# A batched matrix product: output stores joined two by two, on the semaphores of the first loads

## Chip, core and metric

The kernel runs on one core of one Trainium2 chip. The metric is the device time of one execution in microseconds, as a median of several. Profiles are of one execution each; the profile's span is some 1.7 us shorter than the time of the same execution (before: 121.65 us of 123.40 us). Kernels are compared only within the same rounds. PE is TensorE, DVE VectorE, ACT ScalarE, POOL GpSimd, and SP the sync engine, which issues all DMAs.

## The reference

```python
def setup_inputs():
    batch, m, k, n = 16, 512, 512, 512
    return {"a": np.random.randn(batch, k, m).astype(np.float32),
            "b": np.random.randn(batch, k, n).astype(np.float32)}

def reference(a, b):
    return np.matmul(a.transpose(0, 2, 1), b).astype(np.float32)
```

Two inputs of 16.8 MB each come in and one output of 16.8 MB goes out, 50.33 MB in all.

## The kernel before

Batches are handled in eight pairs. A pair's a and b are loaded in fp32 (2 MB each, four buffers), cast to bf16 by DVE, multiplied by PE into PSUM, and copied by ACT into one of seven output buffers (such a copy is called an eviction). The eighth pair reuses the first output buffer, so ACT waits there for the first store. SP issues every load, then every store, on one queue.

```python
out_v = out.rearrange("(pair g) (c t) n -> pair c g t n", g=G, t=T)   # G = 2, T = 4
NO = pairs - 1                                                        # 7 output buffers
o_ts = [pool.tile([P, G, T, N], f32, name=f"o{j}") for j in range(NO)]
# ... loads; the last one is issued in two halves, the first of them on s_h
nc.sync.wait_ge(s_h, 16)
for i in range(pairs - 1):
    nc.sync.wait_ge(s_out, i + 1)              # ACT has finished pair i
    nc.sync.dma_start(out_v[i], o_ts[i % NO][:]).then_inc(s_o if i else s_o0, 16)
# ... casts on DVE, matmuls on PE
for i in range(pairs):                         # ACT
    if i == NO:
        nc.scalar.wait_ge(s_o0, 16)            # first store landed: buffer 0 is free
    # ... four copies PSUM -> o_ts[i % NO], then s_out += 1
with tc.tile_critical(sync_engine=mybir.EngineType.Pool, no_gpsimd_drain=True):
    nc.gpsimd.wait_ge(s_o0, 16)
    nc.gpsimd.wait_ge(s_o, 16 * (pairs - 2))
tc.no_sync_barrier()
nc.sync.dma_start(out_v[pairs - 1], o_ts[(pairs - 1) % NO][:])        # final store
```

## Time and profile before

| what | value |
|---|---|
| time, median of 3 runs | 123.24 us (123.08 to 123.38) |
| span of the profiled execution | 121.65 us |
| busy share: PE, DVE, ACT | 53%, 31%, 26% |
| share of the 16 DMA engines' span filled with packets | 97.8% |
| DMAs: loads, stores | 19, 8 |
| data packets: 16 KB (loads), 8 KB (part of the loads, all stores) | 1664, 2816 |

What matters in the table is not how busy a compute engine is, but that the DMA engines have no idle time to give back. Every DMA also writes one small semaphore packet on each of the 16 engines; 27 DMAs make the 432 small packets of the page. Below, a boundary is the place on one engine where one DMA's semaphore packet ends it and the next DMA's data begin, and the receipt is the time from the last of these packets to the complete semaphore.

### The profile page before, as it was taken

Reading aid. Unit: us, or ns where it says so; the run is one execution under the profiler, and the core shown is the slowest. Engines: PE = TensorE matmul, PEld = TensorE weight load, DVE = VectorE, ACT = ScalarE, POOL = GpSimd, SP = SyncE. Lnnn points to the kernel's source line nnn. Section 1 sums busy time; section 2 is a strip of 40 time slices with the busy share of each in tenths; the row PEclk is TensorE's granted clock in tenths of the full one; section 3 lists DMA queues with packets and bytes.
Section 4 is the critical chain, followed back from the end, with each engine's and each line's share of the span. In section 5 each row is a group of like instructions: output and inputs, shape, how many; then the busy total and the mean of one; then the engine's idle time right before and its main releaser. Section 6 shows DMA issues by size and latency. Waiting matters only on the chain. (4 is left out here: it accounts for less than half of the span.)

```text
span 121.7 us, 1207 instructions
## 1 busy us (share of the span) xinstructions
PE 65.0 (53%) x480; PEld 35.6 (29%) x480; DVE 38.0 (31%) x48; ACT 32.2 (26%) x41; POOL 0.2 (0%) x4
## 2 busy tenths in 40 slices
PE   0007937919989759739969919999930000000000
PEld 0002302306646336414536605556610000000000
DVE  0051061095684094082464446266000000000000
ACT  4000330330390840840191480065190000000000
POOL 0000000000000000000000000000000000000000
PEclk9999996799999999976999996899999555555555
DMA  3999999999999999999999999999999999999993
GB/s 59 428 428 426 463 431 431 431 431 436 431 431 431 431 431 431 431 431 431 431 431 431 431 431 399 431 420 423 426 428 423 428 431 431 431 431 428 431 428 162
DMA packets 4912, 50.33 MB, mean 414 GB/s; under 512 B 432, under 2 KB 432, under 8 KB 432
## 3 DMA queue, kind: packets, MB, share of 16 engines
q1 hardware_dynamic: 4912, 50.33, 97.8%
HBM read 33.55 MB, written 16.78 MB: 414 GB/s over the span
## 5 line engine op out<-in xcount | busy, mean ns | idle before, releaser
L151 PE MATMUL ps<-bbf,abf 64*128 64x512 bf16 x448 | 53.1, 394 | 11.9 <-PEq L146 11.9
L151 PEld LDWEIGHTS ps<-bbf,abf 64*128 64x128 bf16 x448 | 31.4, 113 | 33.7 <-issue 19.2
L176 ACT COPY o<-ps 128x1024 f32<-128x1024 f32 x28 | 26.3, 1026 | 39.3 <-PE ps L151 39.3
L113 DVE CAST abf<-x 128x2048 bf16<-128x2048 f32 x14 | 17.2, 1225 | 20.6 <-PE ps L151 14.9
L113 DVE CAST bbf<-x 128x2048 bf16<-128x2048 f32 x14 | 17.1, 1224 | 11.8 <-DMA x<-in_b_dram 11.8
L131 PE MATMUL ps<-bbf,abf 128*128 128x512 bf16 x32 | 11.9, 554 | 12.5 <-PEq L129 12.5
L131 PEld LDWEIGHTS ps<-bbf,abf 128*128 128x128 bf16 x32 | 4.3, 138 | 19.6 <-issue 19.1
L170 ACT COPY o<-ps 128x1024 f32<-128x1024 f32 x4 | 4.1, 1014 | 19.2 <-PE ps L131 19.2
L94 DVE CAST abf<-x 128x2048 bf16<-128x2048 f32 x2 | 2.5, 1228 | 12.7 <-PE ps L131 6.9
L94 DVE CAST bbf<-x 128x2048 bf16<-128x2048 f32 x2 | 2.5, 1226 | 1.2 <-DMA x<-in_b_dram 1.2
L181 ACT ACTIVATE done<-done 1x1 uint32<-1x1 uint32 x8 | 1.6, 197 | 0.0
L170 ACT ACT_TABLE_LOAD x1 | 1.3, 1283 | 0.9 <-SPq L69 0.9
L119 DVE MEMSET done<- 1x1 f32 x14 | 0.8, 59 | 0.0
L98 DVE MEMSET done<- 1x1 f32 x2 | 0.1, 59 | 0.0
L203 POOL MEMSET const-uint8-127<- 128x1 uint8 x1 | 0.1, 103 | 0.0
L203 POOL MEMSET const-bfloat16-1.0<- 128x1 bf16 x1 | 0.1, 102 | 0.0
L203 POOL MEMSET const-float32-0.0<- 128x1 f32 x1 | 0.1, 99 | 0.2 <-issue 0.2
L203 POOL MEMSET const-float32-1.0<- 128x1 f32 x1 | 0.1, 99 | 0.0
## 6 DMA issues: line engine op xcount, KB each, us to landing
out_dram<-o SPq DMA_DIRECT2D x8, 2048.0 KB, 22.2
x<-in_a_dram SPq DMA_DIRECT2D x7, 2048.0 KB, 12.1
x<-in_b_dram SPq DMA_DIRECT2D x6, 2048.0 KB, 15.6
x<-in_b_dram SPq DMA_DIRECT2D x4, 1024.0 KB, 12.1
x<-in_a_dram SPq DMA_DIRECT2D x2, 1024.0 KB, 6.8
```

The costliest lines, as they stand in the source:

```text
L94: nc.vector.tensor_copy(out=bf_ts[0][:], in_=x_ts[j][:, u * RV:(u + 1) * RV, :]).then_inc(s_cast, 1)
L98: nc.vector.memset(dve_done[:, j:j + 1], 0.0).then_inc(s_in, 1)
L113: nc.vector.tensor_copy(out=(bbf_ts if n % 2 else abf_ts)[v][:], in_=x_ts[n % NX][:, v * RV:(v + 1) * RV, :],).then_inc(s_cast, 1)
L119: nc.vector.memset(dve_done[:, n:n + 1], 0.0).then_inc(s_in, 1)
L131: mm = nc.tensor.matmul(ps_ts[0][h][:, t % 2, :], a_m[:, r, t], bbf_ts[0][:, r, :], start=(r == 0), stop=(r == RV - 1),)
L151: mm = nc.tensor.matmul(ps_ts[g][h][:, t % 2, :], a_m[:, t], bbf_ts[v][rows, r, :], start=(v == 0 and r == 0), stop=(v == V - 1 and r == R ...
L170: nc.scalar.copy(out=o_ts[0][:, g, 2 * h:2 * h + 2, :], in_=ps_ts[0][h][:]).then_inc(s_ev[h], 1)
L176: ev = nc.scalar.copy(out=o_ts[i % NO][:, g, 2 * h:2 * h + 2, :], in_=ps_ts[g][h][:])
L181: nc.scalar.memzero(act_done[:, i:i + 1]).then_inc(s_out, 1)
L203: nc = _bacc.Bacc("TRN2", target_bir_lowering=False, num_devices=1)
```

## The change

Its intent is fewer and larger DMAs (two pairs, 4 MB, per store) and two semaphores fewer: the stores count on the semaphores on which the first two loads landed. The output buffers become slices of one tile, so that two neighbours are contiguous in a partition.

```diff
-    out_v = out.rearrange("(pair g) (c t) n -> pair c g t n", g=G, t=T)
+    out_v = out.rearrange("batch (c t) n -> c batch t n", t=T)
...
-    o_ts = [pool.tile([P, G, T, N], f32, name=f"o{j}") for j in range(NO)]
+    o_t = pool.tile([P, NO, G, T, N], f32, name="o")
+    o_ts = [o_t[:, j] for j in range(NO)]
...
     s_f = [tc.alloc_semaphore(f"s_f{j}") for j in range(2)]
+    s_o0, s_o = s_f
-    s_o0 = tc.alloc_semaphore("s_o0")
-    s_o = tc.alloc_semaphore("s_o")
...
-        for i in range(pairs - 1):
-            nc.sync.wait_ge(s_out, i + 1)
-            nc.sync.dma_start(out_v[i], o_ts[i % NO][:]).then_inc(s_o if i else s_o0, 16)
+        for i in range(0, NO, 2):
+            n = min(2, NO - i)
+            nc.sync.wait_ge(s_out, i + n)
+            nc.sync.dma_start(
+                out_v[:, G * i:G * (i + n)],
+                o_t[:, i:i + n].rearrange("p i g t n -> p (i g) t n"),
+            ).then_inc(s_o if i else s_o0, 16)
...
-                nc.scalar.wait_ge(s_o0, 16)
+                nc.scalar.wait_ge(s_o0, 32)
...
-        nc.gpsimd.wait_ge(s_o0, 16)
-        nc.gpsimd.wait_ge(s_o, 16 * (pairs - 2))
+        nc.gpsimd.wait_ge(s_o0, 32)
+        nc.gpsimd.wait_ge(s_o, 16 * ((NO + 1) // 2))
...
-    nc.sync.dma_start(out_v[pairs - 1], o_ts[(pairs - 1) % NO][:])
+    nc.sync.dma_start(out_v[:, batch - G:batch], o_ts[(pairs - 1) % NO])
```

## The prediction

> **What bounds the kernel now.** I began with the page's slices. The rows below are TensorE, ScalarE, the mean busy share of the 16 DMA engines in tenths, and what they moved. The reader is to see that the compute engines are idle for the last quarter, and that the DMA row has no hole between its first and last slice.
>
> ```profile
> PE   0007937919989759739969919999930000000000
> ACT  4000330330390840840191480065190000000000
> DMA  3999999999999999999999999999999999999993
> GB/s 59 428 428 426 463 431 431 431 431 436 431 431 431 431 431 431 431 431 431 431 431 431 431 431 399 431 420 423 426 428 423 428 431 431 431 431 428 431 428 162
> ...
> q1 hardware_dynamic: 4912, 50.33, 97.8%
> ```
>
> The queue line puts one number on it: packets occupy 97.8% of the span, on one queue, for 50.33 MB. What the change can win is therefore not in PE, DVE or ACT, but in (a) the two ends of the span and (b) whatever the queue loses between one DMA and the next. The second view was the time line of the issuing engine (SP), together with the waits of that engine. Columns of the time line: start, duration, line, operation.
>
> ```profile
> 65.72 0.43 SPq L82 DMA_DIRECT2D x<-in_b_dram  x1
> 78.82 10.87 SPq L87 DMA_DIRECT2D out_dram<-o  x7
> 91.68 2.63 SPq L188 DMA_DIRECT2D out_dram<-o  x1
> ...
> SPq L214 <- DMA out_dram<-o: 26.3, 1, 26.3
> SPq L87 <- DMA x<-in_b_dram: 12.6, 1, 12.6
> SPq L87 <- ACT done L181: 0.5, 1, 0.5
> ```
>
> The loads are all issued by 66.2 us. SP then waits 12.6 us for the first half of the last load, issues seven stores back to back from 78.82 us, and the eighth at 91.68 us. After that, SP sits 26.3 us waiting for that eighth store to land: in the last quarter the kernel only drains a queue that was filled long before. The view of the output tensor gives issue times (least, median, greatest, in ns):
>
> ```profile
> L87 SPq DMA_DIRECT2D out_dram<-o x7: 403/1262/4927, 78.8 to 84.8; - x7
> L188 SPq DMA_DIRECT2D out_dram<-o x1: 2628/2628/2628, 91.7 to 91.7; - x1
> DMA to landing us min/median/max: 7.5/22.2/31.1
> ```
>
> An issue costs 0.40 us when the queue has room, and up to 4.93 us when it must wait for room. 4.93 us is one store's own transfer time: the sequencer is held up by a full queue, the queue is not held up by the sequencer. The third view was a table of stretches; the last two columns are DMA share and rate.
>
> ```profile
> 3.00:78.00 75.00, 53.98 (x384) 29.02 (x386) 33.25 (x42) 23.24 (x30) 0.00 (x0) 0.93 1.01 430
> 81.00:86.00 5.00, 4.65 (x44) 2.68 (x42) 2.37 (x4) 2.92 (x5) 0.00 (x0) 1.00 0.99 419
> 86.00:91.00 5.00, 3.38 (x32) 1.97 (x28) 0.00 (x0) 3.28 (x4) 0.00 (x0) 1.00 1.03 434
> 101.00:106.00 5.00, 0.00 (x0) 0.00 (x0) 0.00 (x0) 0.00 (x0) 0.00 (x0) 0.50 1.02 433
> 106.00:111.00 5.00, 0.00 (x0) 0.00 (x0) 0.00 (x0) 0.00 (x0) 0.00 (x0) 0.50 1.02 431
> ```
>
> The load phase runs at 430 GB/s and five-microsecond stretches of the store phase at 419 to 434 (stretches this short scatter with the packets that happen to cross their edges). So loads of 2 MB and stores of 2 MB both keep the engines full, with a DMA boundary every 4.9 us.
>
> Finally I read the trace's packet records themselves. One DMA engine starts an 8192 B data packet every 306 ns. At the end of each store it writes one 4 B semaphore packet, and the next data packet starts **6 ns** after that one (80.541 us, then 80.547 us on the engine that ends its loads first). Boundaries on one engine are 4.900 us apart, again and again (85.441, 90.341, 95.241 us): 16 packets at 305.9 ns, 4.894 us, and 6 ns. That is the whole visible cost of a DMA boundary.
>
> **What the Trainium skill says.** "DMA: Bandwidth & Descriptors", section "Anatomy of one DMA", gives a fixed cost of about 2 us per DMA (fitted on the GpSimd path), mostly the receipt of the last write, and says that the semaphore write itself is a bubble of about one cycle. The trace agrees on the second point (6 ns). The receipt is there too, but short and hidden: the last semaphore packet starts at 120.333 us and the semaphore is complete at 120.708 us, 0.375 us, and between stores it runs beside the next store's data. "SBUF — State Buffer", section "The DMA setup-cost knee", advises coalescing into the largest transfer; its formula for 2 MB would give 2 + 4.81 = 6.8 us, but here stores come 4.90 us apart, because the DMAs are queued. That rule is the change's intent and does not apply here. "DMA: Bandwidth & Descriptors", section "Where 436 GB/s comes from", has a ceiling of 435 GB/s; the trace's 431 GB/s is within 1% of it, so a larger DMA has next to no rate left to gain. The section on why a DMA increments its semaphore by 16 warns of two DMAs in flight on one semaphore. Here the first loads have long landed (5.8 and 8.2 us) before a store adds to the same semaphores (after 85 us), and every wait is for the full sum (32, or 64 for one load and three stores), so the reuse is safe and costs no time.
>
> **The change part by part.**
> Stores: in place of seven loop stores there are three of 4 MB and one of 2 MB; the final 2 MB store stays, so eight DMAs become five. On the DRAM side each partition still has runs of 4 x 512 floats, 8192 B, as in the trace's records of the stores; only four such runs instead of two belong to a partition. So I keep 2048 data packets of 8192 B and 128 per engine. Removed: 3 boundaries x 6 ns = **0.02 us** on every engine. Removed from SP: three issues of 0.4 to 1.3 us, off the path.
> Start of the stores: the first 4 MB store needs the output of pairs 0 and 1, ready long before. The wait for the first half of the last load still comes last and passes at 78.82 us. At the kernel's start the first data packet followed its issue by 1.02 us (0.942 to 1.961 us). A store issued at 78.82 us could thus move data from 79.84 us, and the first engine to finish its loads gets to it at 80.541 us: 0.7 us of slack. Issues of 128 packets took 0.33 to 0.44 us and of 256 packets 0.40 us, so I take 0.5 us, 0.8 at most, for 512, which fits in the slack. Cost 0.
> ScalarE: its last four evictions reuse the first output buffer and wait for the first store. That landed at 86.32 us, before the matmuls were ready at 87.67 us. After the change they wait for a store of 4 MB, which lands where the second store lands today, 91.42 us. The evictions move from 87.72 to about 91.5 us, take 3.76 us as today, and the final store is issued at about 95.5 us instead of 91.68. Its first data packet is due at about 115 us, when four loop stores (14 MB) have drained. Slack: some 18 us. Cost 0.
> Semaphores: two fewer. The one instruction that clears them all at the end takes 0.16 us; I count at most 0.01 us for two.
> End: the slowest engine's last packet, the receipt (0.375 us), and the closing barriers (0.94 us from 120.708 to the span's end) stay. Sum: -0.02 - 0.01 = **-0.03 us**, so 123.21, rounded to **123.2 us**.
>
> **The rivals.**
> First, *each DMA pays a fixed cost in the open*. If the 2 us of the skill were paid at every boundary, three fewer would give about 6 us, 117 us. Against it: next data 6 ns after the semaphore packet, on all engines. If only the 0.375 us receipt were paid, 1.1 us and 122.1 us; the same records speak against it.
> Second, *a new hole between loads and stores*. If descriptors of a 4 MB store take twice as long and start only when all are made, the slack of 0.7 us could be used up. At 1.3 us of issue (the worst of the stores that waited in part) it would be overrun by about 0.2 us: 123.4 us.
> Third, *the late eviction becomes the bound*. This needs 18 us of further delay; I see nothing that would make it. Were the store and eviction serialised at the end, the final 2 MB would stand alone: some 5 us, 128 us.
> Fourth, *one engine's luck*. From the last boundary of the loads, 80.900 us, eight stores of 4.900 us end at 120.100 us. Fifteen engines keep that schedule; one, which should have ended at 120.033, ends at 120.333 us, since its packets between 83 and 92 us took 315 to 352 ns instead of 309. That is 0.23 us on the end of the span, in the stretch in which SP issues into a full queue. With other issues this can vanish (123.0 us) or grow (123.4 us). It is larger than all that the change removes.
> Fifth, *other addresses of the writes*: a partition's four runs lie in four batches, 1 MB apart, instead of two. Two at the same distance run at full rate today; I give a slower write of some per cent a chance of one in fifty.
>
> **Range and chances.** The three runs of before lie within 0.3 us. The fourth rival gives 0.2 us either way, the second 0.2 upwards. The range is 122.95 to 123.5 us. A change of 2% would be 2.5 us, which only the first rival (down) or the third and fifth (up) could make: 0.01 and 0.02; same 0.97.
>
> **What would show it right or wrong.** Right: 2048 store packets still of 8192 B and 48 fewer small ones; DMA packets near 97.8% of the span and no dip between 80 and 82 us; the last evictions at about 91.5 us and the final issue at about 95.5 us with the end unmoved; landings of 4 MB stores some 9.8 us apart. Wrong: store packets of another size or longer than 309 ns throughout; a stretch with idle DMA engines near 81 us or 115 us; a final store that starts after the queue has run dry.

## The result

The kernel after took 123.19 us (median of 6 runs, 123.09 to 123.41), the kernel before, in the same rounds, 123.26 us (6 runs, 123.08 to 123.38). The ratio is 0.9998, with a 95% interval from 0.9985 to 1.0011: the same time. Ratios and intervals here are from the same rounds alone; they are not quite the ratios of the medians quoted.

The page of the kernel after has these rows: ACT, the DMA engines' busy share and rate by slice, and the queue's sum.

```profile
ACT  4000423302900920390560084190009200000000
...
DMA  2999999999999999999999999999999999999994
GB/s 57 424 432 429 467 432 432 432 432 432 432 432 432 432 432 427 432 432 416 432 427 427 432 432 402 432 427 427 429 429 432 429 429 432 421 424 429 429 424 208
...
q1 hardware_dynamic: 4864, 50.33, 97.7%
```

Still no hole in the DMA row between the ends. 48 packets fewer (4864 for 4912), which is the three removed DMAs times 16 engines, and the same bytes. In the ACT row the last evictions stand about a slice further right than before.

The time line of SP (start, duration, line, operation) and its waits:

```profile
65.65 0.43 SPq L83 DMA_DIRECT2D x<-in_b_dram  x1
78.75 8.98 SPq L89 DMA_DIRECT2D out_dram<-o  x4
95.04 0.37 SPq L193 DMA_DIRECT2D out_dram<-o  x1
```

```profile
SPq L219 <- DMA out_dram<-o: 24.9, 1, 24.9
...
SPq L89 <- DMA x<-in_b_dram: 12.6, 1, 12.6
```

The stores still go out when the first half of the last load has landed (78.75 us). Only the final store moved, from 91.68 to 95.04 us, and since the queue had room by then, it took 0.37 us to issue in place of 2.63. SP's wait for it is 24.9 us in place of 26.3, because it begins later and the span is 0.3 us shorter. The issue times of the stores (least, median, greatest, ns), and ACT's last copies on the time line (the bracket is the idle time before them and what ended it):

```profile
L89 SPq DMA_DIRECT2D out_dram<-o x4: 403/688/5502, 78.8 to 82.2; - x4
L193 SPq DMA_DIRECT2D out_dram<-o x1: 372/372/372, 95.0 to 95.0; - x1
...
DMA to landing us min/median/max: 12.3/25.4/33.3
```

```profile
91.09 3.76 ACT L181 COPY o<-ps 128x1024 f32<-128x1024 f32 x4 [8.88 <-DMA out_dram<-o]
94.71 0.20 ACT L186 ACTIVATE done<-done 1x1 uint32<-1x1 uint32 x1
```

The first 4 MB store takes 403 ns to issue, as the first 2 MB store did. ACT now waits 8.88 us for that store, and it costs nothing: the final store, which waits for ACT, is issued at 95.04 us and has to stand in the queue until 115 us in any case. A few stretches of the kernel after (us, then PE, PEld, DVE, ACT and POOL busy, granted clock, DMA share, GB/s):

```profile
3.00:78.00 75.00, 52.33 (x399) 29.54 (x401) 34.48 (x43) 23.24 (x30) 0.00 (x0) 0.95 1.01 431
...
81.00:86.00 5.00, 5.00 (x49) 3.09 (x47) 1.52 (x4) 1.21 (x3) 0.00 (x0) 1.00 1.02 433
86.00:91.00 5.00, 1.67 (x16) 0.83 (x12) 0.00 (x0) 0.00 (x0) 0.00 (x0) 1.00 1.00 424
```

Loads and stores run at the rates of before; the scatter of the store stretches is that of packets at their edges.

The packet records say it exactly. On one engine a 4 MB store takes 9.794 us from semaphore packet to semaphore packet, against 2 x 4.900 = 9.800 us for two 2 MB stores. The change removes 6 ns per removed boundary.

### The profile page after: what moved, and what is told of

Its sections match the earlier page's. It is cut to its first block, busy times and chain, and to the rows that moved or that the text cites. A ratio compares the mean times of both kernels' runs of the same rounds, so it can differ in the third digit from the quotient of the medians.

```text
span 121.4 us, 1204 instructions
## 1 busy us (share of the span) xinstructions
PE 61.7 (51%) x480; PEld 35.0 (29%) x480; DVE 38.1 (31%) x48; ACT 32.2 (27%) x41; POOL 0.2 (0%) x4
## 2 busy tenths in 40 slices
DMA packets 4864, 50.33 MB, mean 415 GB/s; under 512 B 384, under 2 KB 384, under 8 KB 384
## 3 DMA queue, kind: packets, MB, share of 16 engines
q1 hardware_dynamic: 4864, 50.33, 97.7%
## 4 chain that ended last, share of the span: by engine, by line
DMA 63%; DVE 6%; issue 3%; ACT 2%; SPq 2%; ACTq 1%
DMA x<-in_b_dram 53%; DMA out_dram<-o 10%; DVE bbf L118 3%; DVE abf L118 3%; ACT o L181 2%; SPq L74 1%; ACTq L70 1%; SPq L72 1%; SPq L80 0%; DVE done L124 0%; ACT done L186 0%; SPq L219 0%; SPq L70 0%
## 5 line engine op out<-in xcount | busy, mean ns | idle before, releaser
L181 ACT COPY o<-ps 128x1024 f32<-128x1024 f32 x28 | 26.3, 1026 | 45.9 <-PE ps L156 37.0
L136 PE MATMUL ps<-bbf,abf 128*128 128x512 bf16 x32 | 8.7, 433 | 12.4 <-PEq L134 12.4
L136 PEld LDWEIGHTS ps<-bbf,abf 128*128 128x128 bf16 x32 | 3.7, 121 | 16.9 <-issue 14.8
```

What stands on the lines that cost most here:

```text
L136: mm = nc.tensor.matmul(ps_ts[0][h][:, t % 2, :], a_m[:, r, t], bbf_ts[0][:, r, :], start=(r == 0), stop=(r == RV - 1),)
L181: ev = nc.scalar.copy(out=o_ts[i % NO][:, g, 2 * h:2 * h + 2, :], in_=ps_ts[g][h][:])
```

## Experiments

**Theory:** the kernel's time is the DMA queue's, a boundary between two queued DMAs costs 6 ns, and all other effects of the change have slack. **Rivals:** each DMA pays its completion in the open; the larger first store leaves a hole after the loads; the later eviction becomes the bound; single slow packets of one engine move the end, because SP issues into a full queue. Each kernel is the kernel before or after with the edit shown (the counts waited for on the store semaphores are adapted, which is not always shown); all gave correct results. The time after "beside" and the ratio refer to the kernel before in the same rounds.

### The semaphores alone (a_sem_only)

```diff
     s_f = [tc.alloc_semaphore(f"s_f{j}") for j in range(2)]
+    s_o0, s_o = s_f
-    s_o0 = ...; s_o = ...            # and the waits raised by 16 each
```

> The kernel before with the second part of the change alone: the store semaphores are those of the first loads, eight stores of 2 MB stay. Theory (the queue sets the time and no semaphore lies on its path): same, 123.2 us, within 0.1 us of before; the clearing instruction at the end at most 0.01 us shorter. Rival (a shared semaphore delays something, or fewer semaphores shorten the end): a difference above 0.2 us.

Measured: 123.39 us (5 runs) beside 123.36 us of before (9 runs), ratio 1.0001 (0.9988 to 1.0015). The clearing instruction took 161 ns in the kernel before and 158 ns in the kernel after. Within this interval the semaphores cost and win nothing.

### The 4 MB stores alone (b_4mb_only), and two repeats (after2, b2_4mb_only)

```diff
-    s_o0, s_o = s_f
+    s_o0 = tc.alloc_semaphore("s_o0")
+    s_o = tc.alloc_semaphore("s_o")   # and the waits lowered by 16 each
```

> The kernel after with its own store semaphores back: the 4 MB stores alone. Theory (a boundary between DMAs costs 6 ns of each engine): same, 123.2 us, with 27 DMAs less 3 and the slowest engine at its schedule of 9.794 us per 4 MB. Rival (each DMA's receipt is paid in the open, hidden in the change by a loss elsewhere that the semaphores cause): 1.1 us faster than before.

Measured: 123.18 us beside 123.36 us, ratio 0.9987 (0.9973 to 1.0001). The 1.1 us of the open receipt are excluded, but 0.13% is more than 0.02 us. So this kernel and the kernel after were run again, on one chip in the same rounds.

> The kernel after once more, with five rounds. The 4 MB stores alone came out 0.13% faster than before, with an interval that just holds 1. Theory (6 ns per boundary; the rest is which engine meets slow packets): within 0.1% of before, 123.2 us. Rival (4 MB stores are really some 0.2 us faster): 0.15% below before here and in the repeat of the 4 MB stores alone.

> The 4 MB stores with their own semaphores once more, on the same chip as the repeat of the kernel after. Theory: within 0.1% of before. Rival (a real gain of the 4 MB stores): again 0.13% or more below before.

Measured: the kernel after 123.25 us, ratio 0.9996 (0.9982 to 1.0010); the 4 MB stores with their own semaphores 123.19 us, ratio 0.9986 (0.9973 to 1.0000); before 123.33 us (9 runs). Neither text is met in full: the stores with their own semaphores were again 0.14% below before, outside the theory's 0.1%, while the kernel after, with the very same stores, was 0.04% below. Each interval alone just reaches 1, but both runs, on two chips, gave the same 0.13 to 0.14%, and all ten executions took 123.28 us or less. So a gain of some 0.15 us is more likely real than noise. The three boundaries give 0.02 us of it; the rest, and why the kernel after does not show it, stays unexplained. It is small beside the 2% (2.5 us) that would count.

### More DMAs instead of fewer (c_1mb)

```diff
-            nc.sync.dma_start(out_v[i], o_ts[i % NO][:]).then_inc(...)
+            for g in range(G):
+                nc.sync.dma_start(out_v[i][:, g], o_ts[i % NO][:, g]).then_inc(...)
```

> The kernel before with each loop store split by batch: fourteen stores of 1 MB and the final one of 2 MB, 15 stores in place of 8, packets still 8192 B. Theory of 6 ns per boundary: 7 x 6 ns = 0.04 us more, so 123.3 us, same. Rival of the open receipt (0.375 us per DMA): 2.6 us more, 125.8 us. Rival of 2 us per DMA: 14 us more.

Measured: 123.44 us beside 123.36 us, ratio 1.0013 (0.9999 to 1.0027). Seven more DMAs do not cost 2.6 us, let alone 14. On one engine the 1 MB stores are 2.453 us apart: eight packets at 305.9 ns and again 6 ns. The view of the output tensor shows what the sequencer does with it:

```profile
L88 SPq DMA_DIRECT2D out_dram<-o x14: 347/1218/1246, 78.8 to 93.2; - x14
L189 SPq DMA_DIRECT2D out_dram<-o x1: 831/831/831, 94.9 to 94.9; - x1
```

The typical issue takes 1.2 us, since the queue is full, and all the same the time is unchanged: SP has 2.45 us per store.

### More and smaller packets (h_4kb)

```diff
+            for h in range(H):
                 nc.sync.dma_start(
-                    out_v[:, G * i:G * (i + n)],
+                    out_v[:, G * i:G * (i + n), 2 * h:2 * h + 2],
-                    o_t[:, i:i + n].rearrange(...),
+                    o_t[:, i:i + n, :, 2 * h:2 * h + 2].rearrange(...),
                 ).then_inc(...)
```

> The kernel after with each loop store split by halves of a partition's rows: runs of 4096 B in place of 8192, so 1792 more data packets, 112 more on each engine, in eight loop DMAs and a final one. Theory (what costs is a packet, not a DMA): from 16 KB packets (607 ns apart, from 4.862 us per 2 MB load) against 8 KB packets (305.9 ns apart) one packet more costs about 4.8 ns, so 112 x 4.8 = 0.54 us more than after: 123.7 us. Rival (neither DMA count nor packet size matters at this rate): 123.2 us.

Measured: 123.73 us; the 4 MB stores of the same rounds took 123.18 us, so 0.55 us for 0.54 expected. Against before the ratio is 1.0029 (1.0016 to 1.0043). The page's packet and queue lines:

```profile
DMA packets 6721, 50.33 MB, mean 413 GB/s; under 512 B 449, under 2 KB 449, under 8 KB 4033
...
q1 hardware_dynamic: 6720, 50.33, 98.2%
```

The queue has 1856 packets more than in the kernel after: 1792 of data, and 64 semaphore packets of four more DMAs. 2 MB in 4 KB packets take 4.975 us on an engine (32 x 155.3 ns and 6 ns), in 8 KB packets 4.900 us: 4.7 ns for each packet more. The length of a contiguous run in the output is what cost time here, and the change leaves that at 8192 B.

### A first store of 8 MB (d_8mb) and of 12 MB (e_12mb)

```diff
-        for i in range(0, NO, 2):
-            n = min(2, NO - i)
+        for i, n in [(0, 4), (4, 3)]:        # d_8mb;  e_12mb: [(0, 6), (6, 1)]
```

> The kernel after with stores of four and three pairs (8 MB and 6 MB) and the final 2 MB. Theory (the wait of the last eviction for the first store has slack): the first store lands at about 100.9 us, the final store is issued at about 104.9 us and its data are due at 114.8 us, so no loss: 123.2 us. Rival (a late eviction costs time): a later end in proportion, some 10 us.

> The kernel after with one store of six pairs (12 MB), one of 2 MB and the final 2 MB. Theory: the first store lands at about 110.6 us, the final store is issued 3.98 us later as in the kernel after, at 114.6 us, and its first data come 1.02 us later, at 115.6 us; the engines run dry from 114.8 to 115.2 us, so a hole of some 0.5 to 0.9 us opens: 123.7 to 124.1 us. Rival (slack is larger, since data are handed on before the whole store has landed): 123.2 us.

Measured for 8 MB: 123.30 us beside 123.32 us, ratio 1.0000 (0.9985 to 1.0015). ACT's last copies and the final issue came another 10 us later than in the kernel after, at no cost:

```profile
101.16 3.76 ACT L180 COPY o<-ps 128x1024 f32<-128x1024 f32 x4 [18.83 <-DMA out_dram<-o]
...
105.12 0.37 SPq L192 DMA_DIRECT2D out_dram<-o  x1
```

Measured for 12 MB: 123.74 us, ratio 1.0037 (1.0021 to 1.0052). Now the slack is used up. The time line, then the stretches around 115 us:

```profile
110.80 3.76 ACT L180 COPY o<-ps 128x1024 f32<-128x1024 f32 x4 [26.91 <-DMA out_dram<-o]
...
114.75 0.37 SPq L192 DMA_DIRECT2D out_dram<-o  x1
```

```profile
113.00:115.00 2.00, 0.00 (x0) 0.00 (x0) 0.00 (x0) 1.61 (x3) 0.00 (x0) 0.50 0.93 393
115.00:115.60 0.60, 0.00 (x0) 0.00 (x0) 0.00 (x0) 0.00 (x0) 0.00 (x0) 0.50 0.04 14
115.60:118.00 2.40, 0.00 (x0) 0.00 (x0) 0.00 (x0) 0.00 (x0) 0.00 (x0) 0.50 1.03 437
```

The final store is issued at 114.75 us, as worked out beforehand; between 115.0 and 115.6 us the engines move next to nothing (DMA share 0.04), and the first packets of the final store start at 115.64 us. This is the third rival, real, but three times as far away as the change goes.

### The first store issued too late (f_late_first) and very early (i_early, j_one_early)

```diff
-        nc.sync.wait_ge(s_h, 16)
+        nc.sync.wait_ge(s_x[(2 * pairs - 1) % NX], 16 * (2 * pairs // NX))   # f_late_first
                                       # i_early: the line is taken away
+            if i: nc.sync.wait_ge(s_h, 16)                                   # j_one_early: in the loop
```

> The kernel after, in which the first store is issued only when the last load has landed in full (81.2 us) and not its first half (78.7 us). Theory (a store's data come 1.0 us after its issue, and only the early issue hides that): first data at about 82.2 us, loads drained at 80.5 to 80.9 us, so a hole of 1.4 to 1.7 us: 124.7 us. Rival (the engines work on at once, or the store phase is not what sets the end): 123.2 us.

Measured: 124.76 us beside 123.32 us, ratio 1.0122 (1.0107 to 1.0138). Stretches around the end of the loads, first of the kernel after, then of this one:

```profile
78.00:80.50 2.50, 2.15 (x22) 1.20 (x20) 1.57 (x2) 2.11 (x3) 0.00 (x0) 1.00 1.05 442
80.50:82.20 1.70, 1.70 (x16) 0.95 (x16) 1.70 (x3) 1.70 (x3) 0.00 (x0) 1.00 0.95 400
```

```profile
80.50:82.20 1.70, 1.70 (x16) 0.97 (x16) 1.70 (x3) 1.70 (x3) 0.00 (x0) 1.00 0.11 43
82.20:84.00 1.80, 1.80 (x18) 1.18 (x18) 0.33 (x2) 0.02 (x1) 0.00 (x0) 1.00 1.01 410
```

The 0.95 of the kernel after is no hole: the stretch before it has 1.05, the kernel before has 1.07 from 80.5 to 82.2 us, and in the packet records data follow each semaphore packet there within 6 ns. In this run the engines stand at 0.11 from 80.5 to 82.2 us, and each of them has a gap of 1.27 to 1.56 us, for 1.4 to 1.7 expected. The store was issued at 81.231 us and its first data packet started at 82.175 us, 0.94 us later. So the second rival's hole exists when the lead is missing; the change keeps the lead, and its 4 MB store is issued as fast as one of 2 MB.

> The kernel after without the issuing engine's wait for the first half of the last load before the first store, so that the first stores queue up right behind the loads. Theory (the lead of 2.4 us is already enough, the queue works in order): 123.2 us, no dip at 81 us and none before. Rival (a store's data delay the last loads or the queue's room is taken from them): later last loads and a longer time. If the lead were still too short, this would be faster.

Measured: 124.17 us beside 123.33 us, ratio 1.0071 (1.0057 to 1.0085). The theory's expectation failed here. The stretches:

```profile
78.00:80.50 2.50, 2.50 (x26) 1.70 (x24) 2.05 (x2) 0.36 (x1) 0.00 (x0) 1.00 1.02 334
80.50:82.20 1.70, 1.36 (x14) 0.61 (x10) 0.61 (x2) 1.70 (x3) 0.00 (x0) 1.00 0.98 400
```

Packets fill the engines (share 1.02), yet they move only 334 GB/s from 78 to 80.5 us: single 8 KB packets of the last half load took up to 872 ns for 309, and that load was complete at 82.20 us instead of 81.18. After that the stores ran on the usual schedule. The last test asked whether it takes all the stores.

> As the kernel after, with the first 4 MB store alone issued right behind the loads (at about 66.2 us) and the others after the first half of the last load as before. The early issue of all stores cost 0.9 us, in packets of the last half load that took up to 0.87 us between 78.9 and 81 us. If one store waiting in the queue behind the last load is enough for that: 124.2 us and long packets again. If it takes a queue that is filled to the brim: 123.2 us and no long packets there.

Measured: 123.84 us (6 runs, 123.56 to 124.02) beside 123.30 us, ratio 1.0051 (1.0038 to 1.0063), with packets of up to 612 ns between 79.2 and 81 us. One waiting store is enough for the larger part of the loss; a full queue is not needed. It lies between the two expectations. Why a store that was issued some 15 us before its turn (66.2 us, for loads that end at 81.2) slows the load ahead of it, and one issued 2.4 us before does not, stays open. The wait that looks idle in SP's row (12.6 us) is thus worth 0.9 us (124.17 beside 123.25 us of the kernel after in the same rounds), and both kernels have it.

### At most two stores in flight (g_paced)

```diff
             nc.sync.wait_ge(s_out, i + 1)
+            if i >= 2:
+                nc.sync.wait_ge(s_os[i - 2], 16)     # a semaphore for each store
```

> The kernel before with at most two loop stores in flight: each store waits for the landing of the last but one, on a semaphore of its own. No store is then issued into a full queue. Theory (two stores of 2 MB are deep enough): 123.2 us, every issue at 0.4 to 0.5 us. If the full queue is what slowed single packets of one engine between 83 and 92 us, no store packet is longer than 309 ns here and the time is up to 0.2 us lower (123.0 us); if slow packets stay, they have another cause.

Measured: 123.34 us beside 123.32 us, ratio 1.0002 (0.9988 to 1.0016). Issue times and times to landing:

```profile
L88 SPq DMA_DIRECT2D out_dram<-o x7: 372/372/468, 78.9 to 106.0; - x7
...
DMA to landing us min/median/max: 7.4/9.7/13.8
```

No loop store waits for room any more, and the time is the same: two stores of 2 MB are deep enough. But the slow packets stay: 16 of them between 83.6 and 90.9 us. They come without any issue into a full queue.

### Slow packets in all profiles

From the packet records: the slowest engine's last boundary of the loads, the end that the steady store times (4.900 us per 2 MB, 9.794 us per 4 MB, 2.453 us per 1 MB) give from there, the start of the last semaphore packet as it was, and the store packets over 309 ns after 81 us with the sum of their excess.

| run | loads end | scheduled end | real end | late by | slow packets |
|---|---|---|---|---|---|
| before | 80.900 | 120.100 | 120.333 | 0.233 | 23, 0.32 us |
| after | 80.878 | 120.060 | 120.061 | 0.001 | 16, 0.21 us |
| after2 | 80.899 | 120.081 | 120.219 | 0.138 | 22, 0.31 us |
| b2_4mb_only | 80.935 | 120.117 | 120.236 | 0.119 | 18, 0.20 us |
| a_sem_only | 80.922 | 120.122 | 120.313 | 0.191 | 37, 0.54 us |
| b_4mb_only | 80.845 | 120.027 | 120.156 | 0.129 | 23, 0.31 us |
| c_1mb | 80.932 | 120.174 | 120.173 | -0.001 | 27, 0.41 us |
| d_8mb | 80.998 | 120.168 | 120.321 | 0.153 | 16, 0.21 us |
| g_paced | 81.044 | 120.244 | 120.244 | 0.000 | 16, 0.21 us |

An 8 KB packet takes 309 ns as a rule, and the next one starts 305.9 ns after it. The runs with a hole or a late load are left out, and so is h_4kb, whose packets are smaller (they too are slow between 82 and 87.5 us, up to 176 ns for 159). Every one of these executions has slow packets that begin at 81.6 to 83.9 us. The end comes 0 to 0.23 us late; as I read the records, it depends on whether an engine that meets them is one of the last anyway. In the kernel before, the late engine ended its loads at 80.833 us, 0.07 us before the last one; in the kernel after, it was the one that ended them first (80.450 us), and its 0.19 us of delay did not reach the end. A delay of 0.23 us is about as large as the spread of the times of one kernel, and thirteen times the 0.018 us of the three boundaries.

## Why the prediction was right

The prediction was 123.2 us, and 123.19 us was measured; the kernel before had 123.24 us when it was made and 123.26 us in the rounds of the result. That the two figures meet to 0.02 us is luck, since the runs of one kernel spread over 0.3 us. What is shown is that the time stays the same. By the prediction's own steps:

- **The cost of a boundary, 6 ns.** Shown by the records; the prediction takes it to agree with a bubble of about one cycle, but the trace has no cycles, only the 6 ns. 4 MB stores take 9.794 us, 1 MB stores 2.453 us, and seven DMAs more did not cost what a receipt in the open would (c_1mb). That the 4 MB stores alone came out some 0.15 us faster is more than this step allows, and open. The receipt of 0.375 us is that of the last store; between the stores of the kernel before it took up to 0.53 us, beside the next data all the same.
- **Packets of unchanged size.** Shown: 4864 packets are 4912 less 48, and what a changed size would have cost is shown by the 4 KB runs, 0.55 us. The other addresses (the fifth rival) did not slow them: the median packet takes 309 ns in both kernels.
- **The start of the stores.** Right in substance; the size was too cautious. The issue of the first 4 MB store took 0.403 us, not 0.5 to 0.8. (The range the estimate began with was misread: issues of 128 packets took up to 0.48 us, one 0.65 us, not 0.44.) From the issue to the first data 0.94 us were measured in f_late_first, for the 1.02 us taken over from the first load. The slack is then 80.45 - (78.75 + 0.94) = 0.76 us, for 0.7 stated.
- **The late eviction.** ACT's copies at 91.09 us and the final issue at 95.04 us, for 91.5 and 95.5 predicted. The estimate had taken the landing of the second store of before (91.42 us), 0.36 us after the landing now measured (91.07 us); some 0.2 us of this is the slow engine's delay. That the slack is real and finite is shown by 8 MB (no cost) and 12 MB (0.4 us).
- **The semaphores.** 3 ns less for the clearing, within the 10 ns allowed; no effect alone (a_sem_only).
- **One engine's luck.** The two profiled spans differ by 121.65 - 121.35 = 0.30 us. Of it, 0.233 - 0.001 = 0.23 us is the slow engine, which in the kernel after had time to spare, 0.022 us is an earlier end of the loads, 0.028 us a shorter last receipt (0.375 and 0.347 us), and 0.018 us the boundaries. The medians do not show the 0.23 us; I take it, without having shown it, that this is because other executions of both kernels draw other lots, as the table's rows do. The prediction placed these packets in the stretch in which SP issues into a full queue; that link fell with g_paced. Their cause is open. (In the kernel before they took 313 to 352 ns; the prediction has 315 for the least.)

What the prediction did not see is that an earlier first store would have hurt. It touches no step, since the change leaves the moment of that issue alone.

## What to carry to other kernels

Before joining DMAs, look at the gap between one DMA's semaphore packet and the next one's data: in a queue that is never empty it was 6 ns here, and then the number and length of the packets counted for more than the number of DMAs. A larger store also frees its buffer later; work out when the next writer needs it and when the queue would run dry, for this is where joining begins to cost. The moment of the first store after the last load is worth tuning both ways: 2.5 us later cost 1.2%, 12.6 us earlier 0.7%.

## What the Trainium skill lacked or had wrong

- "SBUF — State Buffer", section "The DMA setup-cost knee": it charges every transfer some 2 us, and does not set apart DMAs that stand in a queue. For queued DMAs the runs show 6 ns per DMA and times within 0.3 us of each other for stores from 1 MB to 8 MB (123.44, 123.36, 123.18 and 123.30 us for 1, 2, 4 and 8 MB, the last on another chip). A single transfer that is waited for was not tested.
- "DMA: Bandwidth & Descriptors", section "Anatomy of one DMA": it puts most of about 2 us on the write receipt, on the GpSimd path. On this queue, the last store's receipt took 0.34 to 0.41 us in the profiles, and the receipts of the kernel before up to 0.53 us.
- No page that I found: a store queued some 15 us ahead behind loads slows the last load (packets up to 872 ns for 309; 0.5 to 0.9 us on the time), while one queued 2.4 us ahead does not.
- "DMA: Bandwidth & Descriptors", section "Why small descriptors are slow (HBM only)": it has an overhead per packet in cycles, but no time for one more packet at these sizes. The runs show 4.7 ns between 8 KB and 4 KB.
- No page that I found explains the slow packets (up to 352 ns for 309) that begin at 81.6 to 83.9 us in every profile of the table, where SP issues all DMAs.
